# A hybrid decoder trunk on one core: token-major projections in wider passes, HGRN2 operands one step earlier, attention in one run, 1/rms turned by transfers

## The chip, the core and the metric

The kernel runs on one core of a Trainium2 chip. Five engines work side by side, each through its own queue of instructions in a fixed order: PE multiplies matrices into PSUM (eight banks of 128 partitions by 512 fp32 values), DVE works elementwise and reduces, ACT applies functions and copies with a scale, POOL fills constants and issues some of the transfers, SP issues the rest. The metric is the device time of one execution in microseconds, lower is better. A difference counts as measured from about 0.2%.

## The reference

Two layers over 512 tokens of width 1024, in fp32. Each layer has a half-step SwiGLU feed-forward, one combined projection whose columns feed three token mixers, one output projection, and a second half-step feed-forward:

```python
x = x + 0.5 * swiglu(rms_norm(x, ffn1_norm[l]), ffn1_w_in[l], ffn1_w_out[l])
h = rms_norm(x, mix_norm[l]) @ w_mix_in[l]
(c_x, c_b, c_c, h_q, h_f, h_i, h_g, f_q, f_k, f_v, f_f) = jnp.split(h, split_at, axis=-1)
y = jnp.concatenate([short_conv_mixer(...), hgrn2_mixer(...), fox_mixer(...)], axis=-1)
x = x + y @ w_mix_out[l]
x = x + 0.5 * swiglu(rms_norm(x, ffn2_norm[l]), ffn2_w_in[l], ffn2_w_out[l])
```

- The short convolution is causal, three taps over 256 channels: `b_gate * conv3(c_gate * x_in)`.
- HGRN2 has 4 heads of 64 by 64 and works in chunks of 64 tokens: a state per head decays by a forget gate per channel and takes up k v, and within a chunk every query sees earlier keys under the decay between them. Its output is normalised per head and multiplied by silu of a gate.
- FoX is causal attention with 8 heads of 64; q and k are normalised per head by their rms, the logits get the difference of cumulative log forget gates, and a softmax over the row follows.

## The kernel before

The residual stream stands in SBUF with features on partitions (`xT`, 8 tiles of 128 features by 512 tokens). Every fp32 operand of a dense product is split into a rounded high part (ACT, lines 334 and 732) and a low rest (DVE, lines 335 and 734), and a product is three matmuls: high by high, high by low, low by high (`mm3`, lines 346, 352, 353). The split weights stand in `hl`, of which there are three, filled from `st`, of which there are two. The norm's gain is in the operand; the factor 1/rms, `inv`, is applied to the products.

A dense product is streamed by `stream_steps`: two rows of weight tiles are loaded and split (a granule), multiplied for all accumulators (jobs), and then it yields, so that other work can be written between its steps. In the last granule it goes job by job, so that banks are finished one after the other.

The framework lists every engine's instructions by the order in which they are written and by its own estimate of when they are ready; `high_priority` lets the weight splits go ahead. The order on each engine is fixed when the program is built; dense matmuls can have been put ahead of a block that was written earlier and was not expected to be ready. PSUM's eight banks are named `mm` (three), `sc` (two), `pt` (two) and `po` (one), and a bank is given again when its readers are done.

The mixer of a layer (`mix`, line 926) runs like this:

1. Features by tokens: the forget logits, the gate and the q of HGRN2 (`features`, weights stationary, 512 tokens moving). The norm's sum is taken in the first one, and `inv` follows.
2. `inv` is also needed with tokens on partitions (`invc`, and `inv2` = `invc` squared over 64). Four one-column matmuls of `inv`'s first row with a 1 turn it (lines 997 to 1004).
3. HGRN2's v and the FoX forget logits, tokens by features, 264 columns in four banks (line 1019). `invc` scales them (lines 1027, 1030).
4. `hgrn` runs for two head pairs as two generators taken in turn. Its steps are gates, decayed keys, state sums and scan, then seven levels. At each level the elementwise operands `e` and `e2` are made, a block of fp32 matmuls gives the scores into an `sc` bank, and a masked copy (line 1290) puts them into `A`. Then follow the outputs in `po` (lines 1301, 1308) and their norm.
   Between these steps stand the steps of the FoX projections (`fox_qkv`): q, k and v of heads 0 to 3, then of heads 4 to 7, each a pass of 256 columns with two token blocks per bank (`tokens`), 4 steps of 24 matmuls. After q and k, each bank is squared, summed by head, and multiplied by its 1/rms out of PSUM (lines 1368 to 1376); v is split out of PSUM (lines 1382, 1383).
5. Attention, heads 0 to 3 (`fox_attend`), beside the convolution's projections (12 steps); then heads 4 to 7 as a new run, beside three quarters of the output projection (`most`, 12 steps). A head has four items, one for each block of 128 queries: scores three items ahead, softmax, transposes, products with V one item later. `beside` takes one dense step at each item from the third on, and what is left after the run. The order of the rows of the output projection is HGRN2 (2, 3), heads 0 to 3 (4, 5), convolution (0, 1), and after attention heads 4 to 7 (6, 7).

Loads of weights go by SP's queue. POOL's queue holds small loads at the mixer's start, the memsets of `q2` and of `S2` in HGRN2, and the ones for attention's operands.

## Time and profile before

| | us |
|---|---|
| median of 3 runs | 1847.46 (1845.98 to 1848.6) |
| the profiled execution | 1847.27 |
| its span | 1845.3 |
| granted TensorE clock | 1.0 throughout |
| projections beside HGRN2, layer 0 and layer 1 | 93.5 and 92.8 |
| attention, layer 0 and layer 1 | 110.2 and 110.4 |

A row of the table by windows gives a stretch, its length, and for each engine its busy time and its instructions. A row of the groups gives line, engine and operation, the tiles written and read, shape and count, then busy time, mean duration of one in ns, and the idle time ahead of them with what ended it. A row of the timeline gives start, duration, engine and line. A matmul's duration overlaps the next one's, so what one costs is read from start to start. The fp32 matmuls of HGRN2 stand as two rows each, so "x8" is a block of four.

### The profile page before, as it was taken

Reading aid. Unit: us, or ns where it says so; the run is one execution under the profiler, and the core shown is the slowest. Engines: PE = TensorE matmul, PEld = TensorE weight load, DVE = VectorE, ACT = ScalarE, POOL = GpSimd, SP = SyncE. Lnnn points to the kernel's source line nnn. Section 1 sums busy time; section 2 is a strip of 40 time slices with the busy share of each in tenths; the row PEclk is TensorE's granted clock in tenths of the full one; section 3 lists DMA queues with packets and bytes.
Section 4 is the critical chain, followed back from the end, with each engine's and each line's share of the span. In section 5 each row is a group of like instructions: output and inputs, shape, how many; then the busy total and the mean of one; then the engine's idle time right before and its main releaser. Section 6 shows DMA issues by size and latency. Waiting matters only on the chain.

```text
span 1845.3 us, 33378 instructions
## 1 busy us (share of the span) xinstructions
PE 1826.9 (99%) x13532; PEld 1698.6 (92%) x13532; DVE 1476.5 (80%) x2101; ACT 1005.9 (55%) x1462; POOL 182.5 (10%) x186
## 2 busy tenths in 40 slices
PE   8999999999999999999999999999999999999999
PEld 6899999899877899999889999998998788999997
DVE  7889787678787988879678887966868878888883
ACT  4455554564665555555445555545546665555552
POOL 0011120100000101112001111201000001020210
PEclk9999999999999999999999999999999999999999
DMA  7658783332323767868276787823323238677762
GB/s 205 183 126 194 178 177 92 69 96 72 76 75 98 215 136 175 186 169 172 81 201 139 169 188 184 172 61 89 81 64 87 81 103 228 151 158 195 150 137 91
DMA packets 247529, 254.00 MB, mean 138 GB/s; under 512 B 19632, under 2 KB 232112, under 8 KB 247376
## 3 DMA queue, kind: packets, MB, share of 16 engines
q1 hardware_dynamic: 191664, 183.69, 33.4%
q0 software_dynamic: 55712, 68.18, 23.2%
q8 instruction: 106, 1.74, 0.4%
q14 instruction: 47, 0.39, 0.1%
HBM read 226.08 MB, written 2.10 MB: 124 GB/s over the span
## 4 chain that ended last, share of the span: by engine, by line
PE 91%; DVE 4%; ACT 3%; issue 1%; DMA 1%; SPq 0%; ACTq 0%; DVEq 0%
PE mm L346 13%; PE mm L353 13%; PE mm L352 13%; PE sc L346 6%; PE sc L353 6%; PE sc L352 6%; PE pt L346 6%; PE pt L352 6%; PE pt L353 6%; PE po L346 3%; PE po L352 3%; PE po L353 3%; PE po L1449 1%; DVE hl L335 1%; ACT hl L334 1%
## 5 line engine op out<-in xcount | busy, mean ns | idle before, releaser
L732 ACT CAST hl<-w 128x1024 fp32r<-128x1024 f32 x322 | 337.7, 1050 | 346.9 <-PE mm L353 81.7
L734 DVE TENSOR_TENSOR hl<-w,hl 128x1024 fp32r<-128x1024 f32 x322 | 392.7, 1220 | 86.5 <-ACT hl L732 86.4
L335 DVE TENSOR_TENSOR hl<-st,hl 128x512 fp32r<-128x512 f32 (+2 forms) x196 | 166.5, 851 | 118.3 <-ACT hl L334 117.3
L334 ACT CAST hl<-st 128x512 fp32r<-128x512 f32 (+2 forms) x196 | 146.6, 750 | 206.9 <-PE mm L353 67.4
L346 PE MATMUL mm<-xc,hl 128*128 128x256 f32 (+1 forms) x730 | 201.3, 276 | 0.3 <-ACT g L831 0.3
L353 PE MATMUL mm<-xc,hl 128*128 128x256 f32 x728 | 201.2, 276 | 0.0
L352 PE MATMUL mm<-xc,hl 128*128 128x256 f32 x728 | 201.1, 276 | 0.0
L346 PE MATMUL sc<-xc,hl 128*128 128x256 f32 (+1 forms) x530 | 146.3, 277 | 0.6 <-ACT g L831 0.6
L353 PE MATMUL sc<-xc,hl 128*128 128x256 f32 x528 | 146.0, 277 | 0.0
L352 PE MATMUL sc<-xc,hl 128*128 128x256 f32 x528 | 145.9, 276 | 0.0
L346 PEld LDWEIGHTS mm<-xc,hl 128*128 128x128 f32 x730 | 137.1, 188 | 0.8 <-ACT g L831 0.5
L353 PEld LDWEIGHTS mm<-xc,hl 128*128 128x128 f32 x728 | 136.7, 188 | 0.1
L352 PEld LDWEIGHTS mm<-xc,hl 128*128 128x128 f32 x728 | 136.7, 188 | 0.0
L352 PE MATMUL pt<-xc,hl 128*128 128x256 f32 x480 | 132.6, 276 | 0.0
L346 PE MATMUL pt<-xc,hl 128*128 128x256 f32 (+1 forms) x482 | 132.6, 276 | 0.0
L353 PE MATMUL pt<-xc,hl 128*128 128x256 f32 x480 | 132.5, 276 | 0.0
L346 PE MATMUL mm<-hl,x 128*128 128x256 f32 (+1 forms) x384 | 112.4, 293 | 0.7 <-DVE ft L442 0.3
L346 PE MATMUL mm<-x,hl 128*128 128x512 f32 x272 | 109.7, 403 | 0.0
L353 PE MATMUL mm<-hl,x 128*128 128x256 f32 (+1 forms) x384 | 107.6, 280 | 0.0
L352 PE MATMUL mm<-hl,x 128*128 128x256 f32 (+1 forms) x384 | 107.3, 279 | 0.0
L353 PE MATMUL mm<-x,hl 128*128 128x512 f32 x272 | 106.5, 392 | 0.0
L352 PE MATMUL mm<-x,hl 128*128 128x512 f32 x272 | 106.0, 390 | 0.0
(470 smaller groups left out, 5677.1 us busy)
## 6 DMA issues: line engine op xcount, KB each, us to landing
w<-in_ffn_w_in_dram SPq DMA_DIRECT2D x140, 512.0 KB, 5.7
w<-in_ffn_w_out_dram SPq DMA_DIRECT2D x64, 512.0 KB, 4.4
w<-in_ffn_w_out_dram POOLq DMA_DIRECT2D x56, 512.0 KB, 8.9
st<-in_w_mix_in_dram SPq DMA_DIRECT2D x88, 256.0 KB, 2.7
w<-in_ffn_w_in_dram POOLq DMA_DIRECT2D x39, 512.0 KB, 8.4
st<-in_ffn_w_in_dram SPq DMA_DIRECT2D x72, 256.0 KB, 3.3
w<-S POOLq DMA_DIRECT2D x35, 512.0 KB, 4.7
st<-in_ffn_w_out_dram SPq DMA_DIRECT2D x24, 512.0 KB, 4.1
```

The lines of the kernel that those rows point to most:

```text
L334: a = nc.scalar.copy(hi, src[:, c : c + w])
L335: b = nc.vector.tensor_sub(lo, src[:, c : c + w], hi)
L346: i = nc.tensor.matmul(acc[:, c], ah, bh[:, c], start=first and c.start == 0, stop=False, skip_group_check=True,)
L352: nc.tensor.matmul(acc, ah, bl, start=False, stop=False, skip_group_check=True)
L353: i = nc.tensor.matmul(acc, al, bh, start=False, stop=last, skip_group_check=True)
L732: A(nc.scalar.copy(hi, src))
L734: return lambda: V(nc.vector.tensor_sub(lo, src, hi))
L1449: nc.tensor.matmul(self.ob[:, t0 + u * P : t0 + 2 * P], V[:, j, h % 4].rearrange("p a d -> p (a d)"), part[:, j, u:, :].rearrange("p i t - ...
```

## The change

- `stream_steps` gets `wide`: the first granule goes job by job as the last one does, and every granule yields in its middle too.
- `tokens` makes one pass of 512 columns over four banks (three `mm` and `po`), one token block in each: q and k of heads 0 to 3 together, q and k of heads 4 to 7, then v of all heads. Each pass has 4 granules of 48 matmuls with 512 moving columns, 8 half-passes in all.
- `fox_qkv` copies a bank of q and k to SBUF with ACT and squares, sums and scales it there. The square goes to a new tile `fs`, of which there is one.
- `hgrn` makes a level's operands one step earlier, behind the matmuls of the level before. Its output accumulates in an `sc` bank, not `po`.
- `invc` comes by two POOL transfers: `inv`'s first row to a DRAM tile, and from there one value a partition. The four matmuls and `ones_r` go.
- `fox_attend` runs once over eight heads. One generator gives the convolution's steps and then those of `most`; a step is taken at the stopping points listed in `BESIDE`. The run stops once more after the first head's preparation and once before its last products. The output projection takes the convolution (0, 1) second and heads 0 to 3 (4, 5) third.

```diff
--- before.py
+++ after.py
@@ -21,6 +21,8 @@
 BANKS = {"mm": 3, "sc": 2, "pt": 2, "po": 1}
 LOOK, LAG = 3, 1
+BESIDE = {0, 1, 2, 33} | {4 + (29 * n) // 20 for n in range(20)}
 P = 128
 T = 512
 D = 1024
@@ -198,6 +200,9 @@
...
+        self.dram = ctx.enter_context(
+            tc.tile_pool(name="dram", bufs=1, space=bass.MemoryType.DRAM)
+        )
...
@@ -216,8 +221,6 @@
...
-        self.ones_r = c.tile([1, 1], F32, tag="ones_r", name="ones_r")
-        nc.vector.memset(self.ones_r, 1.0)
...
@@ -358,7 +361,8 @@
         for _ in self.stream_steps(*args, **kw):
             pass
-    def stream_steps(self, jobs, parts_of, act, nk, mid=None, pre=None, deal=None, keep=False):
+    def stream_steps(self, jobs, parts_of, act, nk, mid=None, pre=None, deal=None, keep=False, wide=False):
@@ -383,12 +387,14 @@
             end = k + kk == nk
             order = (
                 [(job, j) for job in jobs for j in range(kk)]
-                if end
+                if end or wide and k == 0
                 else [(job, j) for j in range(kk) for job in jobs]
             )
             for n, ((acc, cols, toks, *more), j) in enumerate(order):
                 if pre is not None and n == len(order) // 2:
                     pre(k, True)
+                if wide and n == len(order) // 2:
+                    yield
                 ah, al = act(k + j)
                 hi, lo = rows[j]
                 first, last = k + j == 0 and not more, end and j == kk - 1
@@ -967,14 +973,13 @@
...
-            def tokens(a, banks=("mm", "mm")):
-                bs = [self.bank(t) for t in banks]
-                jobs = []
-                for i in range(4):
-                    acc = bs[i // 2][:, 256 * (i % 2) : 256 * (i % 2) + 256]
-                    jobs.append((acc, slice(0, 256), TOK[i]) + ((False,) if i % 2 else ()))
-                yield from self.stream_steps(jobs, cols((a, 256)), self.xact, KD)
+            def tokens(*spans):
+                bs = [self.bank(t) for t in ("mm", "mm", "mm", "po")]
+                yield from self.stream_steps(
+                    [(bk, slice(0, T), t) for bk, t in zip(bs, TOK)], cols(*spans),
+                    self.xact, KD, wide=True,
+                )
                 return bs
             with tc.tile_pool(name=self.n("hg"), bufs=1) as hp:
@@ -994,14 +999,10 @@
...
-                ib = self.bank("pt")
-                for i in range(4):
-                    nc.tensor.matmul(
-                        ib[:, i : i + 1], inv[0:1, TOK[i]], self.ones_r[0:1, 0:1],
-                        start=True, stop=True,
-                    )
                 self.invc, self.inv2 = col("invc", 4), col("inv2", 4)
-                nc.vector.tensor_copy(self.invc, ib[:, 0:4])
+                row = self.dram.tile([1, T], F32, tag="row", name=self.n("row"))
+                nc.gpsimd.dma_start(row, inv[0:1, :])
+                nc.gpsimd.dma_start(self.invc, row.rearrange("o (i p) -> (o p) i", p=P))
...
-                half = [{}, {}]
-                def projections():
-                    for hf in range(2):
-                        yield from self.fox_qkv(mp, hf, tokens, half)
-                dense = projections()
+                half = []
+                dense = self.fox_qkv(mp, hp, tokens, half)
                 step = 0
...
-                def beside(attend, dense):
-                    for n, _ in enumerate(attend):
-                        if n >= 2:
-                            next(dense, None)
-                    for _ in dense:
-                        pass
                 self.begin_norm(next_gain)
-                order = [2, 3, 4, 5, 0, 1, 6, 7]
+                order = [2, 3, 0, 1, 4, 5, 6, 7]
...
-                beside(self.fox_attend(ap_, 0, half[0], qkg), conv())
-                beside(self.fox_attend(ap_, 1, half[1], qkg), most())
+                def dense():
+                    yield from conv()
+                    yield from most()
+                g = dense()
+                for n, _ in enumerate(self.fox_attend(ap_, half, qkg)):
+                    if n in BESIDE:
+                        next(g)
+                    if n == max(BESIDE):
+                        next(g, None)
...
-        yield
         A = own("A", [P, 2, 4, P])
         A8 = A.rearrange("p h i t -> p (h i) t")
+        halves = lambda lev: lambda a, i: a.rearrange(
+            "p (n two w) -> p n two w", two=2, w=2**lev // 2
+        )[:, :, i, :]
+        def operands(lev):
+            w, half = 2**lev // 2, halves(lev)
+            e = tmp()
+            if lev == 0:
+                nc.vector.tensor_mul(e, q, k)
+                return e, None
+            if lev == 1:
+                self.act(half(e, 1), half(lf, 1), AF.Exp)
+                nc.vector.tensor_mul(half(e, 1), half(e, 1), half(q, 1))
+                nc.vector.tensor_mul(half(e, 0), half(e, 1), half(k, 0))
+                return e, None
+            n2 = T // (2 * w)
+            ref = b.rearrange("p (n s) -> p n s", s=2 * w)[:, :, w - 1 : w].to_broadcast(
+                [P, n2, w]
+            )
+            nc.vector.tensor_add(half(e, 0), half(kb, 0), ref)
+            nc.vector.tensor_sub(half(e, 1), half(b, 1), ref)
+            self.act(e, e, AF.Exp)
+            e2 = tmp().rearrange("p (h t) -> p h t", h=2)
+            nc.vector.tensor_mul(
+                e2.rearrange("p h (n w) -> p h n w", w=w),
+                half(e, 1).unsqueeze(1).to_broadcast([P, 2, n2, w]),
+                q2.rearrange("p h (n two w) -> p h n two w", two=2, w=w)[:, :, :, 1, :],
+            )
+            return e, e2
+        ready = operands(0)
+        yield
         for lev in range(7):
-            w = 2**lev // 2
-            half = lambda a, i: a.rearrange("p (n two w) -> p n two w", two=2, w=w)[:, :, i, :]
-            e = tmp()
+            w, half = 2**lev // 2, halves(lev)
+            e, e2 = ready
+            sb = self.bank("sc")
             if lev < 2:
...
                 for i in range(4):
                     nc.tensor.matmul(
                         sb[:, i:8:4], e[:, i * P : (i + 1) * P], self.heads2, start=True, stop=True
                     )
                 d = sb[:, :8].unsqueeze(2)
+                ready = operands(lev + 1)
                 if lev == 0:
                     nc.vector.tensor_mul(
                         A8, self.ident.unsqueeze(1).to_broadcast([P, 8, P]), d.to_broadcast([P, 8, P])
@@ -1265,35 +1291,21 @@
                         )
                 yield
                 continue
...
...
+            if lev < 6:
+                ready = operands(lev + 1)
...
-        ob = self.bank("po")
+        ob = self.bank("sc")
...
-    def fox_qkv(self, mp, hf, tokens, half):
-        nc = self.nc
...
+    def fox_qkv(self, mp, hp, tokens, half):
+        nc = self.nc
+        for hf in range(2):
+            qk = mp.tile([P, 4, 4, 2, HD], F32, tag="qk", name=self.n("qk"), bufs=2)
+            banks = yield from tokens((F_Q + 256 * hf, 256), (F_K + 256 * hf, 256))
+            for i, bank in enumerate(banks):
+                out = qk[:, i].rearrange("p h w d -> p w h d")
+                nc.scalar.copy(out, bank.rearrange("p (w h d) -> p w h d", w=2, h=4))
+                sq = hp.tile([P, 8, HD], F32, tag="fs", name=self.n("fs"))
+                s8 = lambda tag: mp.tile([P, 8], F32, tag=tag, name=self.n(tag), bufs=2)
                 m, r, t = s8("fm"), s8("fr"), s8("ft")
-                nc.scalar.activation(out, src, AF.Square)
-                nc.vector.reduce_sum(m, out, axis=AX.X)
-                bc = lambda c: c[:, 2 * bi : 2 * bi + 2].unsqueeze(2).to_broadcast([P, 2, 4])
-                nc.vector.tensor_mul(m, m, bc(self.inv2))
+                nc.scalar.activation(sq, qk[:, i].rearrange("p h w d -> p (h w) d"), AF.Square)
+                nc.vector.reduce_sum(m, sq, axis=AX.X)
+                nc.vector.tensor_scalar(
+                    m, m, scalar1=self.inv2[:, i : i + 1], scalar2=None, op0=ALU.mult
+                )
                 self.act(r, m, AF.Ln, bias=self.epsc)
                 self.act(r, r, AF.Exp, scale=-0.5)
                 self.rsqrt(r, m, r, t)
-                nc.vector.tensor_mul(r, r, bc(self.invc))
-                nc.vector.tensor_mul(out, src, r.unsqueeze(3).to_broadcast([P, 2, 4, HD]))
...
+                nc.vector.tensor_scalar(
+                    r, r, scalar1=self.invc[:, i : i + 1], scalar2=None, op0=ALU.mult
                 )
-        half[hf] = qk, V
+                out = qk[:, i].rearrange("p h w d -> p (h w) d")
+                nc.vector.tensor_mul(out, out, r.unsqueeze(2).to_broadcast([P, 8, HD]))
+            half.append(qk)
+        V = mp.tile([P, 4, NH, 2, HD], F32R, tag="V", name=self.n("V"))
+        for i, bank in enumerate((yield from tokens((F_V, T)))):
+            src = bank.rearrange("p (h d) -> p h d", d=HD)
+            sc = self.invc[:, i : i + 1]
+            nc.scalar.activation(V[:, i, :, 0, :], src, AF.Copy, scale=sc)
+            nc.vector.scalar_tensor_tensor(
+                out=V[:, i, :, 1, :], in0=src, scalar=sc, in1=V[:, i, :, 0, :],
+                op0=ALU.mult, op1=ALU.subtract,
+            )
+        half.append(V)
     def fox_prep(self, pool, h, qk, g):
@@ -1415,9 +1433,10 @@
         )
         return QA, QB, KA, KB
-    def fox_attend(self, pool, hf, qkv, g):
-        nc = self.nc
-        qk, V = qkv
+    def fox_attend(self, pool, half, g):
+        nc = self.nc
...
-                        V[:, j, h % 4].rearrange("p a d -> p (a d)"),
+                        half[2][:, j, h].rearrange("p a d -> p (a d)"),
...
         late = []
-        heads = range(4 * hf, 4 * hf + 4)
-        items = [(h, i) for h in heads for i in range(4)]
-        ops = {heads[0]: self.fox_prep(pool, heads[0], qk, g)}
-        pb = {it: scores(ops[heads[0]], it[1]) for it in items[:LOOK]}
+        items = [(h, i) for h in range(NH) for i in range(4)]
+        prep = lambda h: self.fox_prep(pool, h, half[h // 4], g)
+        ops = {0: prep(0)}
+        yield
+        pb = {it: scores(ops[0], it[1]) for it in items[:LOOK]}
         for n, (h, i) in enumerate(items):
             yield
-            if i == 0 and h + 1 in heads:
-                ops[h + 1] = self.fox_prep(pool, h + 1, qk, g)
+            if i == 0 and h + 1 < NH:
+                ops[h + 1] = prep(h + 1)
             if n + LOOK < len(items):
                 h2, i2 = items[n + LOOK]
                 pb[h2, i2] = scores(ops[h2], i2)
@@ -1495,8 +1515,10 @@
...
+        yield
         for a in late:
             values(*a[1:])
```

More of the change, by code (lines that the diff above doesn't have):

```diff
@@ L1267, in hgrn @@
                 continue
-            n2 = T // (2 * w)
-            ref = b.rearrange("p (n s) -> p n s", s=2 * w)[:, :, w - 1 : w].to_broadcast(
-                [P, n2, w]
-            )
-            nc.vector.tensor_add(half(e, 0), half(kb, 0), ref)
-            nc.vector.tensor_sub(half(e, 1), half(b, 1), ref)
-            self.act(e, e, AF.Exp)
-            e2 = tmp().rearrange("p (h t) -> p h t", h=2)
-            nc.vector.tensor_mul(
-                e2.rearrange("p h (n w) -> p h n w", w=w),
-                half(e, 1).unsqueeze(1).to_broadcast([P, 2, n2, w]),
-                q2.rearrange("p h (n two w) -> p h n two w", two=2, w=w)[:, :, :, 1, :],
-            )
-            sb = self.bank("sc")
             s2 = sb.rearrange("p (h t) -> p h t", h=2)
@@ L1355, in fox_decay @@
         )
-    def fox_qkv(self, mp, hf, tokens, half):
+    def fox_qkv(self, mp, hp, tokens, half):
         nc = self.nc
-        qk = mp.tile([P, 4, 4, 2, HD], F32, tag="qk", name=self.n("qk"), bufs=2)
-        for w, a in enumerate((F_Q, F_K)):
-            for bi, bank in enumerate((yield from tokens(a + 256 * hf, ("mm", "po" if w and not hf else "mm")))):
-                src = bank.rearrange("p (i h d) -> p i h d", i=2, h=4)
-                s8 = lambda tag: mp.tile([P, 2, 4], F32, tag=tag, name=self.n(tag), bufs=2)
-                out = qk[:, 2 * bi : 2 * bi + 2, :, w, :]
-                m, r, t = s8("fm"), s8("fr"), s8("ft")
-                nc.scalar.activation(out, src, AF.Square)
-                nc.vector.reduce_sum(m, out, axis=AX.X)
-                bc = lambda c: c[:, 2 * bi : 2 * bi + 2].unsqueeze(2).to_broadcast([P, 2, 4])
-                nc.vector.tensor_mul(m, m, bc(self.inv2))
+        for hf in range(2):
[6 more added lines that the diff above has]
+                s8 = lambda tag: mp.tile([P, 8], F32, tag=tag, name=self.n(tag), bufs=2)
+                m, r, t = s8("fm"), s8("fr"), s8("ft")
+                nc.scalar.activation(sq, qk[:, i].rearrange("p h w d -> p (h w) d"), AF.Square)
[3 more added lines that the diff above has]
+                )
                 self.act(r, m, AF.Ln, bias=self.epsc)
```

16 lines of the change are left out of this document (removed).

## The prediction

> **What bounds the kernel now.** I read the page first, its engine line and its chain of work.
>
> ```profile
> PE 1826.9 (99%) x13532; PEld 1698.6 (92%) x13532; DVE 1476.5 (80%) x2101; ACT 1005.9 (55%) x1462; POOL 182.5 (10%) x186
> ...
> PE 91%; DVE 4%; ACT 3%; issue 1%; DMA 1%; SPq 0%; ACTq 0%; DVEq 0%
> ```
>
> PE is both the busiest engine and the chain. So only two things are worth time: matmuls that go away or issue faster, and stretches where PE waits or issues slower than it can. Next I cut the mixer into stretches with the table by windows: projections beside HGRN2 (389 to 483 in layer 0, 1299 to 1392 in layer 1), then attention (483 to 593, 1392 to 1503).
>
> ```profile
> core 0: us, PE busy (x) PEld busy (x) DVE busy (x) ACT busy (x) POOL busy (x), PEclk, DMA share, GB/s
> 389.15:482.69 93.54, 92.05 (x835) 88.48 (x834) 71.14 (x158) 49.00 (x106) 1.86 (x4) 1.00 0.27 69
> 482.69:592.88 110.19, 108.74 (x610) 88.26 (x609) 90.10 (x197) 74.53 (x167) 4.32 (x8) 1.00 0.34 94
> 1299.32:1392.15 92.83, 91.54 (x834) 88.18 (x833) 70.74 (x158) 48.44 (x105) 1.86 (x4) 1.00 0.27 69
> 1392.15:1502.58 110.43, 109.20 (x611) 88.21 (x609) 90.20 (x198) 74.83 (x167) 4.31 (x8) 1.00 0.33 94
> ...
> 403.00:436.00 33.00, 31.93 (x273) 31.42 (x272) 30.51 (x70) 18.38 (x37) 1.86 (x4) 1.00 0.27 68
> 533.00:553.00 20.00, 19.62 (x119) 15.08 (x117) 18.61 (x42) 14.95 (x36) 1.04 (x2) 1.00 0.22 67
> ```
>
> Both layers look alike, so I work out layer 0 and double it. The clock is full everywhere. PE has no idle to speak of (1.5 us in each half), but the last two rows show where another engine comes close: DVE is busy 30.5 of 33 us in the middle of HGRN2 and 18.6 of 20 us around the seam between the two attention runs. The waits of PE in the HGRN2 stretch say the same, all of them on DVE:
>
> ```profile
> PE sc L1287 <- DVE t L1278: 0.8, 2, 0.4
> PE sc L1287 <- DVE fm L1371: 0.3, 1, 0.3
> PE mm L346 <- DVE ft L442: 0.2, 1, 0.2
> PE mm L346 <- DVE qk L1376: 0.2, 1, 0.2
> ```
>
> They sum to 1.5 us a layer.
>
> **The change part by part,** per layer.
>
> 1/rms by transfers. The four one-column matmuls on PE go:
>
> ```profile
> 365.24 0.39 PE L353 MATMUL po<-x,hl 128*128 128x512 f32 x1
> 365.55 1.05 PE L999 MATMUL pt<-ones_r,inv 1*128 1x1 f32 x8
> 366.53 0.50 PE L346 MATMUL mm<-x,hl 128*128 128x512 f32 x1
> ```
>
> From the start of the last matmul before to the first one after is 1.29 us, where the next one would have followed after about 0.23 (12 of them take 2.81, below). That is -1.1. In their place stand two POOL transfers, one waiting for the other; POOL holds nothing behind them but memsets that are needed tens of us later. The nearest row is the small column load on the same queue:
>
> ```profile
> cw<-in_conv_w_dram POOLq DMA_DIRECT2D x6, 1.0 KB, 3.2
> ...
> 355.36 0.69 DVE L446 TENSOR_TENSOR inv<-nr,nt 128x512 f32<-128x512 f32 x1
> ...
> 388.78 0.47 ACT L1027 ACTIVATE v<-mm,invc 128x256 f32<-128x256 f32 x1
> ```
>
> Two in a row are 6.4 us; inv is written at 356.1 and the column form is first read for v at 388.8. The cover is 32.7 us, so I cost the transfers at nothing. What could be late next is the small DVE product inv2 right behind them, if it stands too early in DVE's queue; the weight splits behind it would wait. That is a rival.
>
> Passes of 512 columns. The 24 steps of 24 narrow matmuls become 24 half-passes of 12 wide ones with the same number of multiplications. Here are two narrow steps between HGRN2 blocks, and a wide step between attention items:
>
> ```profile
> 431.45 0.36 PE L346 MATMUL mm<-hl,x 128*128 128x256 f32 x1
> ...
> 434.36 1.06 PE L1287 MATMUL sc<-t,t 128*128 128x128 f32 x8
> 435.17 0.37 PE L346 MATMUL mm<-hl,x 128*128 128x256 f32 x1
> ...
> 438.00 1.05 PE L1287 MATMUL sc<-t,t 128*128 128x128 f32 x8
> ...
> 499.33 0.44 PE L346 MATMUL mm<-x,hl 128*128 128x512 f32 x1
> ...
> 502.14 0.38 PE L1490 MATMUL pt<-ident,P 128*128 128x128 f32 x2
> ```
>
> A narrow step takes 2.91 or 2.83 us, a wide one 2.81, the restart after a foreign block included in each. I take the middle, 2.87 - 2.81 = 0.06 for each of 24: -1.3, with ends of -2.4 (all as the slow ones) and 0. The wide row has the tokens as moving operand, while here the weights move; I assume the same rate.
>
> The Trainium skill, page "TensorE: Matmul & The Clock Gate", section "Back-to-back issue gap", gives N/2.4 + 2.5 ns when warm. By it 24 narrow matmuls take 2.62 us and 12 wide ones 2.59, so this part would be -0.7 and not -1.3; the rows are longer than both, as they hold the restart, and I keep them.
>
> A pass now fills all three mm banks and po, so the next pass needs what the last one has not yet given back. Both outer granules go bank by bank, so a bank is written last three banks before it is reused: 3/4 of a granule of two half-passes, 4.2 us, and at least one HGRN2 block of 0.81. It is freed by one ACT copy, for which the nearest row is the square it stands beside:
>
> ```profile
> L1368 ACT ACTIVATE qk<-mm 128x512 f32<-128x512 f32 x7 | 4.1, 591 | 2.4 <-PE mm L353 2.4
> L1369 DVE TENSOR_REDUCE fm<-qk 128x8 f32<-128x512 f32 x8 | 5.5, 682 | 3.5 <-ACT qk L1368 3.5
> L1371 DVE TENSOR_TENSOR fm<-fm,inv 128x8 f32<-128x8 f32 x8 | 1.3, 162 | 0.1
> L1376 DVE TENSOR_TENSOR qk<-mm,fr 128x512 f32<-128x512 f32 x7 | 4.8, 683 | 0.1
> L1272 DVE TENSOR_TENSOR t<-kb,b 128x256 f32<-128x256 f32 x10 | 4.1, 414 | 0.0
> L1278 DVE TENSOR_TENSOR t<-t,q 128x512 f32<-128x512 f32 x10 | 6.9, 687 | 1.9 <-ACT t L289 1.8
> L1290 DVE COPY_PREDICATED A<-lmask,sc 128x512 f32<-128x512 uint8 x10 | 8.4, 837 | 0.0
> ```
>
> At 0.6 us a copy fits that cover seven times; the eight copies a layer add 4.7 us to an ACT busy 49 of 93.5. I cost them at nothing; if ACT is held up behind a DVE result, PE waits at the pass's first bank. V now comes last and its banks need an ACT and a DVE reading each, while attention prepares its first head; the first product with V comes 12 us after that start, so nothing here either.
>
> Operands one step ahead. This takes the product L1278 out of the wait of L1287. DVE does the same work, so I credit half of the 1.5 us: -0.7, ends -1.5 and 0. Its price is a burst: DVE now normalises four banks at once. A bank is 0.68 + 5 x 0.16 + 0.68 = 2.2 us, so four are 8.7. Over the next two half-passes (2 x 3.66 = 7.3 us with their blocks) DVE also has two HGRN2 steps of 2 x 0.41 + 0.69 + 0.84 = 2.35 each. That is 13.4 us of work in 7.3, a backlog of 6.1, against a lead of one step for each head pair, 7.3 us. The lead covers it, barely; where it does not, dense matmuls can be put ahead of the block. Hence nothing in the sum and a rival below.
>
> One run of attention. The seam is between the last values of heads 2 and 4; a head in the steady part is beside it (PE alone, then the dense matmuls alone):
>
> ```profile
> 528.98:552.07 23.09, 22.71 (x135) 1.00 0.23 69
> 513.95:528.98 15.03, 15.03 (x86) 1.00 0.31 89
> ...
> 528.98:552.07 23.09, 14.57 (x51) 8.80 (x51) 2.74 (x4) 2.44 (x5) 1.00 0.23 69
> 513.95:528.98 15.03, 11.89 (x48) 8.73 (x48) 2.62 (x4) 2.17 (x4) 1.00 0.31 89
> ```
>
> The steady head is 48 dense (4 x 2.81 = 11.24) and 38 others, 3.79 us. At these rates the seam's 51 dense and 84 others take 11.9 + 8.4 = 20.3, not 23.1: 2.8 us are lost there, four items with no dense step to cover DVE. The change spreads 20 dense steps over its stopping points 4 to 31. But DVE's 90.1 us must then fit into some 107 with less slack in each stretch (84% throughout, where the seam has 93%), so I credit 2.0 of 2.8: -2.0, ends -2.8 and 0. The convolution's output is now needed second: its six DVE operations of 0.69 and two ACT ones of 0.6 are 5.3 us, beside one dense step and an item (2.81 + 0.95). Up to 1.6 us could show, which I leave to the upper end, since scores of later items can go first.
>
> Sum: -1.1 - 1.3 - 0.7 - 2.0 = -5.1 a layer, -10.2 for both. The profiled execution took 1847.27 us (span 1845.3 and 2.0 around it), 0.2 below the median of 1847.46. So 1837.1. All gains at their better ends: -7.8 a layer, 1831.7. Only the first term, and the convolution late: +0.5, 1848.3.
>
> **The rivals.**
> Slower: the backlog. If DVE's burst after each of the two QK passes is not covered and no dense work goes ahead, PE waits at the next level's block. For it: 30.5 of 33 us, and all four waits above are on DVE. Against: they are 0.2 to 0.4 us each with two banks at once. Without the wait term the gain is 8.8 us; over four bursts it is eaten at 2.2 us each. With 3.6 each, the price if half the lead is gone, 14.4 - 8.8 = +5.6: 1852.9.
>
> Attention gives nothing, since DVE at 84% everywhere makes PE wait as much in small pieces: 1841.1. For it, the seam shows that DVE, not order, costs the time.
>
> The change does not do what it says: width and lead give nothing as well (a narrow step at 2.83 is a wide one): only -2.2, 1845.1.
>
> The transfers are on the path: two slow landings (8.9 us is the median for large accumulating ones on that queue) with DVE waiting in its queue, 17.8 less two granules of lead (2 x 2.7) are 12.4 a layer: 1861.9 with the other gains.
>
> ```profile
> w<-in_ffn_w_out_dram POOLq DMA_DIRECT2D x56, 512.0 KB, 8.9
> ```
>
> The Trainium skill, page "SBUF — State Buffer", section "SBUF: two separate sides", speaks for this rival: descriptors of POOL's transfers wait while DVE holds the shared port, about 3.1 us instead of 0.62. By that rule two landings would be 6.4 + 5.0, still far inside the cover; no row here shows such a wait.
>
> **How the numbers follow.** Forecast 0.55 (own range 1831 to 1843.5), attention nothing 0.14, only the first term 0.08, backlog 0.18, transfers 0.05. A measurement here tells 0.2% from no change, 3.7 us, so faster is below 1843.8: 0.55 + 0.14 and a little of the third, 0.70. Same 0.10, slower 0.20. The range goes from 1830 (a little under the better ends, for the first head's start, which I did not credit) to 1851, just short of the backlog.
>
> **What would show it.** No one-column matmuls near 366, and the first v scaling still near 388. Half-passes of 12 in about 2.81. Waits of PE on DVE under 1.5 us in HGRN2, and none on ACT's bank copies. No stretch of attention with PE below the steady rate between heads 2 and 4. Wrong would be: a longer projection stretch with waits on DVE at the levels behind a pass, or many small waits in attention.

## The result: 7.0 us less, but not from where it was expected

The changed kernel takes 1840.79 us (median of 6 runs, 1839.53 to 1842.32), the kernel before 1847.80 (median of 6): a ratio of 0.9961, 95% interval 0.9951 to 0.9971. That is 7.0 us faster, inside the range given, 3.7 short of the 1837.1 forecast, and close to the 1841.1 of the rival "attention gives nothing". The profiled execution took 1839.53 us with a span of 1837.8. Its engine line and chain of work:

```profile
PE 1820.7 (99%) x12940; PEld 1668.8 (91%) x12940; DVE 1472.5 (80%) x2066; ACT 1011.6 (55%) x1446; POOL 184.9 (10%) x190
...
PE 92%; DVE 4%; ACT 2%; issue 1%; DMA 1%; SPq 0%; ACTq 0%; DVEq 0%
```

PE has 592 fewer matmuls and is still the bound. The profile after by stages (table by windows; the columns are as before: window, length, then busy time of PE, PEld, DVE, ACT and POOL). Projections beside HGRN2 and attention, layer 0 and layer 1:

```profile
387.71:478.63 90.92, 89.72 (x546) 74.27 (x545) 69.47 (x143) 52.03 (x101) 2.62 (x6) 1.00 0.24 70
478.63:596.74 118.11, 116.74 (x640) 93.92 (x639) 97.53 (x207) 81.35 (x175) 3.44 (x7) 1.00 0.31 88
1294.40:1384.81 90.41, 89.72 (x547) 74.28 (x545) 69.45 (x143) 51.92 (x101) 2.62 (x6) 1.00 0.24 70
1384.81:1502.77 117.96, 116.69 (x640) 93.95 (x639) 97.49 (x207) 81.36 (x175) 3.45 (x7) 1.00 0.31 89
```

The same attention stage of the kernel before, now with its output projection, from the first transposes of the first head to the last matmul on fy:

```profile
482.69:600.49 117.80, 116.16 (x642) 93.97 (x640) 95.36 (x205) 78.88 (x174) 4.32 (x8) 1.00 0.31 88
1392.16:1510.17 118.01, 116.59 (x642) 93.90 (x640) 95.45 (x206) 79.17 (x174) 4.31 (x8) 1.00 0.31 88
```

Stage by stage, in us, measured from PE start to PE start in the two traces:

| stage | before, layers 0 and 1 | after | difference |
|---|---|---|---|
| sum of the norm to the first transposes of HGRN2's keys | 38.19, 38.20 | 37.03, 36.97 | -1.16, -1.23 |
| projections beside HGRN2 | 93.54, 92.84 | 90.92, 90.41 | -2.62, -2.43 |
| attention and output projection | 117.80, 118.01 | 118.11, 117.96 | +0.31, -0.05 |

They sum to -7.2. Everything outside the mixers has the same code in all kernels here; between profiles the stretch between the two mixers still varies by 2.0 us (660.5 to 662.5), so below parts are compared by these stages, and whole kernels by medians.

The projections now run like a metronome. Two HGRN2 blocks with a wide half-pass between them, and two matmuls of the half-pass before (timeline of PE):

```profile
430.03 0.39 PE L355 MATMUL mm<-hl,x 128*128 128x512 f32 x1
...
431.39 0.39 PE L355 MATMUL po<-hl,x 128*128 128x512 f32 x1
...
431.85 1.05 PE L1297 MATMUL sc<-t,t 128*128 128x128 f32 x8
432.66 0.48 PE L349 MATMUL mm<-hl,x 128*128 128x512 f32 x1
...
435.48 1.05 PE L1297 MATMUL sc<-t,t 128*128 128x128 f32 x8
436.28 0.48 PE L349 MATMUL mm<-hl,x 128*128 128x512 f32 x1
```

Each block holds PE for 0.81, each half-pass for 2.82 (2.86 in the first levels). None of the four waits on DVE that the kernel before had here is left. One new wait stands in their place; it is all that the waits of PE list in this stage, first layer 0, then layer 1:

```profile
PE pt L1190 <- ACT t L292: 1.2, 1, 1.2
```

```profile
PE pt L1190 <- ACT t L292: 0.7, 1, 0.7
```

It was in no part of the prediction. The timeline of layer 0 around it, ACT first, then DVE, then PE:

```profile
385.75 0.47 ACT L1028 ACTIVATE v<-mm,invc 128x256 f32<-128x256 f32 x1
388.10 1.05 ACT L337 CAST hl<-st 128x1024 fp32r<-128x1024 f32 x1 [1.89 <-DMA st<-in_w_mix_in_dram]
389.06 0.83 ACT L1028 ACTIVATE v<-sc,invc 128x256 f32<-128x256 f32 x2
...
391.55 0.66 ACT L292 ACTIVATE t<-t 128x512 f32<-128x512 f32 x1
```

```profile
389.19 1.23 DVE L338 TENSOR_TENSOR hl<-st,hl 128x1024 fp32r<-128x1024 f32 x1 [2.13 <-ACT hl L337]
...
390.73 0.68 DVE L1182 TENSOR_TENSOR t<-b,kb 128x512 f32<-128x512 f32 x1
```

```profile
392.26 0.66 PE L1190 MATMUL pt<-ident,t 128*128 128x128 f32 x4 [1.20 <-ACT t L292]
```

ACT takes its instructions in order. At 386 its next one is the cast of a weight granule whose load has not landed; behind that stand the remaining v copies. DVE stands in the same way behind the low part of that granule, and only then computes the exponent of the second head pair's decayed keys (390.73), which ACT exponentiates at 391.55 and PE wants to transpose at 391.1. The kernel before has the same late load (its timeline, ACT and PE):

```profile
388.25 0.62 ACT L334 CAST hl<-st 128x512 fp32r<-128x512 f32 x1 [2.65 <-DMA st<-in_w_mix_in_dram]
...
391.97 0.63 ACT L289 ACTIVATE t<-t 128x512 f32<-128x512 f32 x1 [0.64 <-DVE t L1184]
...
392.66 0.66 PE L1192 MATMUL pt<-ident,t 128*128 128x128 f32 x4
```

There the transposes start right behind the exponential as well, but PE gets to them about 1.5 us later, so that it loses only some 0.2 us (its step in front of them takes 3.15 where the next one takes 2.91). The first gain brought PE there 1.2 us earlier, and the profile after runs 0.3 us ahead at this point; the cast starts only 0.15 earlier.

### The profile page after: what moved, and what is told of

It reads as the page before. It is cut to its first block, busy times and chain, and to the rows that moved or that the text cites. A ratio compares the mean times of both kernels' runs of the same rounds, so it can differ in the third digit from the quotient of the medians.

```text
span 1837.8 us, 32074 instructions
## 1 busy us (share of the span) xinstructions
PE 1820.7 (99%) x12940; PEld 1668.8 (91%) x12940; DVE 1472.5 (80%) x2066; ACT 1011.6 (55%) x1446; POOL 184.9 (10%) x190
## 3 DMA queue, kind: packets, MB, share of 16 engines
q0 software_dynamic: 55840, 68.19, 23.1%
## 4 chain that ended last, share of the span: by engine, by line
PE 92%; DVE 4%; ACT 2%; issue 1%; DMA 1%; SPq 0%; ACTq 0%; DVEq 0%
PE mm L349 13%; PE mm L356 13%; PE mm L355 13%; PE sc L349 6%; PE sc L356 6%; PE sc L355 6%; PE pt L349 6%; PE pt L355 6%; PE pt L356 6%; PE po L349 4%; PE po L355 4%; PE po L356 4%; DVE hl L338 1%; ACT hl L337 1%; PE sc L1297 1%
## 5 line engine op out<-in xcount | busy, mean ns | idle before, releaser
L338 DVE TENSOR_TENSOR hl<-st,hl 128x1024 fp32r<-128x1024 f32 (+2 forms) x172 | 162.9, 949 | 131.5 <-ACT hl L337 131.0
L337 ACT CAST hl<-st 128x1024 fp32r<-128x1024 f32 (+2 forms) x172 | 142.0, 829 | 180.9 <-PE po L356 71.7
L349 PEld LDWEIGHTS sc<-xc,hl 128*128 128x128 f32 x530 | 99.5, 188 | 1.5 <-ACT g L837 1.0
L356 PEld LDWEIGHTS sc<-xc,hl 128*128 128x128 f32 x528 | 99.2, 188 | 0.1
L355 PEld LDWEIGHTS sc<-xc,hl 128*128 128x128 f32 x528 | 99.1, 188 | 0.0
```

The lines of the kernel that those rows point to most:

```text
L337: a = nc.scalar.copy(hi, src[:, c : c + w])
L338: b = nc.vector.tensor_sub(lo, src[:, c : c + w], hi)
L349: i = nc.tensor.matmul(acc[:, c], ah, bh[:, c], start=first and c.start == 0, stop=False, skip_group_check=True,)
L355: nc.tensor.matmul(acc, ah, bl, start=False, stop=False, skip_group_check=True)
L356: i = nc.tensor.matmul(acc, al, bh, start=False, stop=last, skip_group_check=True)
```

## The experiments

First each part of the change alone, in the kernel before. Each run has the kernel before beside it on the same chip (medians 1848.12, 1848.04 and 1849.57 in the three groups below). The changed kernel is in none of these groups, so the runs that start from it are held against it by their ratios to the kernel before, and by the stages of one profile each.

**Transfers alone.** The four one-column matmuls are replaced, nothing else.

```diff
-                    nc.tensor.matmul(ib[:, i : i + 1], inv[0:1, TOK[i]], self.ones_r[0:1, 0:1], ...)
-                nc.vector.tensor_copy(self.invc, ib[:, 0:4])
+                nc.gpsimd.dma_start(row, inv[0:1, :])
+                nc.gpsimd.dma_start(self.invc, row.rearrange("o (i p) -> (o p) i", p=P))
```

> The kernel before with one part alone: 1/rms turned by the two POOL transfers. If the terms add as in the traces (the stretch up to the first decayed-key transpose is 1.16 and 1.23 us shorter after the whole change), this alone gives -2.4 us. If the transfers, or the DVE product behind them, hold something up, the first v scaling stands later than 388.8 us and the gain is under 1 us.

Measured: 1846.79, ratio 0.9991 (0.9982 to 1.0): 1.3 of the expected 2.4, with an interval that reaches no change. The stage of the norm is 1.17 and 1.23 shorter, as expected; the projections behind it are 0.15 and 0.71 longer. In layer 0 the new wait on ACT is already there:

```profile
PE pt L1189 <- ACT t L290: 0.5, 1, 0.5
```

**Wide passes alone.** Narrow passes become passes over four banks; two runs of attention, operands as before.

```diff
-                    acc = bs[i // 2][:, 256 * (i % 2) : 256 * (i % 2) + 256]
+                bs = [self.bank(t) for t in ("mm", "mm", "mm", "po")]
```

> The kernel before with the wide passes alone (q and k copied out of PSUM, v of all heads last, HGRN2's output in an sc bank); HGRN2's operands stay where they were and attention stays in two runs. By width alone: -2.6 us for both layers. Rival: the wait of PE at the second decayed-key transposes that the trace after shows (1.2 and 0.7 us) comes with the larger loads of the wide passes, and the old waits on DVE stay; then the gain is about -2.6 + 1.9 = -0.7 us, and that wait stands in this trace.

Measured: 1845.97, ratio 0.9988 (0.998 to 0.9997). That is 2.15 less, nearer to the 2.6 by width than to the rival's 0.7, but the rival's wait on ACT is there. Projections -1.57 and -0.84, attention +0.01 and +0.22. Waits of PE in the projections of layer 0:

```profile
PE sc L1283 <- DVE ft L447: 0.6, 1, 0.6
PE pt L1188 <- ACT t L289: 0.4, 1, 0.4
PE sc L1283 <- DVE t L1274: 0.3, 1, 0.3
```

**Operands one step ahead alone.**

```diff
+        ready = operands(0)
+            e, e2 = ready
...
+                ready = operands(lev + 1)
```

> The kernel before with HGRN2's operands one step ahead alone. If the old waits of PE on DVE in the levels are the order of the operands, they go: -1.5 us a layer, -3.0 in all. If they are DVE's load (30.5 of 33 us), half of them stay: -1.5 in all or less.

Measured: 1848.30, ratio 1.0 (0.9992 to 1.0009): nothing, where 1.5 or 3.0 were expected. The waits on the products are gone, and one of the same size stands elsewhere:

```profile
PE mm L346 <- DVE V L1397: 1.3, 1, 1.3
```

That is a narrow pass waiting for a bank that DVE has still to empty of V; the step takes 4.33 us where its like take 2.91. The projections are 0.53 and 0.13 shorter than before; without these 1.4 us it would be 1.95 and 1.6. In the kernel before V of the first half comes in the middle of the passes, and DVE, which now does the products first, reaches it later. In the changed kernel V comes last, so this wait has no place there.

**One run of attention alone.**

```diff
-                beside(self.fox_attend(ap_, 0, half[0], qkg), conv())
-                beside(self.fox_attend(ap_, 1, half[1], qkg), most())
+                for n, _ in enumerate(self.fox_attend(ap_, half, qkg)):
+                    if n in BESIDE: next(g)
```

> The kernel before with attention in one run alone (steps at the listed stopping points, convolution second in the output projection). Theory: the time that the seam lost comes back as small losses in every head, since a head with three dense steps leaves PE 12 us where DVE has 10 to 11 us of work: 0 us, within 1. Rival: the join is worth its 2 us a layer, and the change loses it because v comes last in the wide passes; then -4 us here.

Measured: 1850.69, ratio 1.0015 (1.0006 to 1.0024), 2.6 slower, which neither the theory nor its rival had. Projections -0.42 and -0.05, attention +2.06 and +0.70. Two waits of PE are new, here in layer 0; the second is there in layer 1 too:

```profile
PE sc L348 <- ACT fyh L1469: 1.6, 1, 1.6
...
PE mm L348 <- DVE V L1387: 0.4, 1, 0.4
```

The 1.6 is again ACT standing at a cast for a late load, now of the FFN's weights, with the copy behind it that the last rows of the output projection need:

```profile
591.16 1.05 ACT L336 CAST hl<-st 128x1024 fp32r<-128x1024 f32 x1 [3.51 <-DMA st<-in_ffn_w_in_dram]
592.23 0.58 ACT L1465 COPY t<-po 64x512 f32<-64x512 f32 x1
```

Neither wait was taken away by itself in this kernel, so their part in its 2.6 is read from the trace only. The four parts alone sum to -1.33 - 2.15 + 0.18 + 2.57 = -0.7, each with an interval of about 1.7 to either side, where the whole change gives -7.0. They are not terms that can be added: the lead alone uncovers the wait on V, and the one run alone two waits that the whole change does not have. The wait on ACT that shows with the transfers and with the wide passes stays in the whole change.

Then the changed kernel with one thing taken back or mended. **Two runs of attention** in the changed kernel, the rest kept:

```diff
-                for n, _ in enumerate(self.fox_attend(ap_, half, qkg)): ...
+                beside(self.fox_attend(ap_, 0, (half[0], half[2]), qkg), conv())
+                beside(self.fox_attend(ap_, 1, (half[1], half[2]), qkg), most())
```

> The changed kernel with its attention put back into two runs, in the order of the kernel before; the transfers, the wide passes and the operands one step ahead stay. Theory: the loss at the seam only moved into small waits on VectorE, so one run is worth nothing here: 1840.8 within 1.5. Rival 1: the seam's loss did go (2 us a layer) and something else ate it, so two runs are 4 slower: 1845. Rival 2: one run costs what it cost alone (2.6 us), so two runs are faster: 1838.

Measured: 1841.25, ratio 0.9962 (0.9949 to 0.9974), beside 0.9961 for the changed kernel. Attention is 117.92 and 117.85, against 118.11 and 117.96. One run is worth nothing.

**The order of the two casts given.** The second granule of the first pass is cast behind the last v copy, the third behind the exponential of the second pair's decayed keys. Only these two dependencies are added, and on ACT and DVE only the instructions around them change places.

```diff
+                (F_Q + 256 * hf, 256), (F_K + 256 * hf, 256), after={} if hf else {2: "v", 4: "kd"}
...
+            if after is not None:
+                self.tc.add_manual_dep(a.ins, self.last[after], NOSYNC, reason="given order")
```

> The changed kernel, with the order of two weight casts on ScalarE given: the second granule's cast behind the four v copies, the third's behind the exponential of the second head pair's decayed keys. In the trace of the changed kernel this cast waits 1.89 us for its load in front of them, and TensorE's transposes wait 1.2 us (layer 0) and 0.7 us (layer 1). Theory: the in-order queue is what costs these 1.9 us, so they go: 1838.9. Rival: the late load is needed by the next wide step anyway, so the wait only moves there: 1840.8.

Measured: 1837.39, ratio 0.9945 (0.9932 to 0.9957). That is 3.4 less than the changed kernel by the medians and 3.0 by the ratios, whose intervals overlap a little; the stages tell it better. The projections are 89.51 and 89.53, which is 1.41 and 0.88 less: 2.3 in both. The three kernels here that have the casts ordered and the lead kept give 89.50 to 89.53 in all six of these stages. PE has no listed wait left in this stage of either layer. ACT and PE at the place:

```profile
388.61 0.47 ACT L1030 ACTIVATE v<-mm,invc 128x256 f32<-128x256 f32 x1 [0.25 <-PE mm L358]
388.99 1.04 ACT L337 CAST hl<-st 128x1024 fp32r<-128x1024 f32 x1
...
390.53 0.63 ACT L292 ACTIVATE t<-t 128x512 f32<-128x512 f32 x1
```

```profile
391.61 0.60 PE L1193 MATMUL pt<-ident,t 128*128 128x128 f32 x4
```

The half-pass between the two groups of transposes takes 2.84 instead of 4.20. Only the order was changed, so the wait is shown to come from the order of a queue, and the weights are not needed earlier than they come.

**No softmax scaling on VectorE** in three of four items; this kernel leaves out the normalisation of these rows:

```diff
-            nc.vector.reciprocal(rs, rs)
-            if i == 3: ... else: nc.vector.tensor_scalar(pb[:, :n], pb[:, :n], scalar1=rs, ...)
+            if i == 3: nc.vector.reciprocal(rs, rs); ...
```

> The changed kernel without the reciprocal and the scaling of P on VectorE in three of four attention items (the softmax of those rows stays unnormalised: this part of the computation is left out). That takes 8.3 + 24 x 0.16 = 12 us a layer from VectorE's 90. Theory (VectorE is what makes TensorE wait in attention): about half of the 4.3 us of waits that stand outside the steady rhythm go, 2 a layer: 1836.8. Rival (the loss is TensorE's own restarts between foreign matmuls, whatever VectorE does): no change, 1840.8.

Measured: 1840.76, ratio 0.9961 (0.9948 to 0.9973): no change. The same work scaled on ScalarE for the third item only, in the changed kernel:

```diff
-            if i == 3:
+            if i >= 2:
                 nc.scalar.activation(pb[:, :n], pb[:, :n], AF.Copy, scale=rs)
```

> The changed kernel with P of the third item of each head scaled on ScalarE, as it already is for the fourth: 8 x 0.42 = 3.4 us a layer from VectorE to ScalarE (8 x about 0.6). Theory (VectorE is what TensorE waits for): 0.3 to 1 us a layer less, 1839 to 1840. Rival (the length of the chain from score to P counts, and ScalarE's multiply is longer than VectorE's): 1841 to 1843.

Measured: 1840.08, ratio 0.9960 (0.9946 to 0.9974); attention is 0.42 shorter in each layer, too little for the medians to tell. The windows of attention in the kernel without scaling:

```profile
480.65:598.24 117.59, 116.21 (x641) 93.99 (x639) 88.78 (x159) 81.43 (x175) 3.34 (x7) 1.00 0.32 89
1386.12:1503.87 117.75, 116.27 (x641) 93.85 (x639) 88.89 (x159) 81.36 (x175) 3.36 (x7) 1.00 0.32 89
```

DVE is 8.7 us less busy than in the changed kernel (97.5) and the stage is 0.2 to 0.5 shorter. How much DVE has to do sets at most a small part of attention's time. What PE waits for in the changed kernel's attention is this (layer 0):

```profile
PE pt L1510 <- DVE KB L1430: 0.6, 2, 0.3
PE pt L1510 <- DVE PL L1513: 0.2, 1, 0.2
PE po L1468 <- DVE PL L1513: 0.2, 1, 0.2
PE sc L1446 <- ACT P L292: 0.2, 1, 0.2
```

The wait on KB comes twice, at heads 2 and 6. KB is the last reader of the pt bank in which a head is prepared, and these are the two heads whose second item has no dense step in front of it. In the kernel without the scaling, where DVE has less to do, this wait stays (0.5 us in layer 0, here, and 0.6 in layer 1):

```profile
PE pt L1508 <- DVE KB L1430: 0.5, 2, 0.3
```

So, with the casts ordered, **two dense steps moved by one item**:

```diff
-BESIDE = {0, 1, 2, 33} | {4 + (29 * n) // 20 for n in range(20)}
+BESIDE = {0, 1, 2, 33} | {
+    4, 5, 6, 8, 10, 11, 12, 14, 15, 17, 18, 19, 21, 22, 24, 26, 27, 28, 30, 31}
```

The old set has 9 and 25 where the new one has 10 and 26.

> The kernel with the two casts ordered (1837.4), with two of the 24 places of a dense step in attention moved by one item: the one before the first item of heads 2 and 6 goes to before their second item, so that every head's preparation, which holds one of the two pt banks until VectorE has written KB, is followed by a dense step. Theory (a held pt bank makes TensorE wait, 0.3 us at each of these two heads, whatever VectorE's load): 0.6 a layer goes, 1836.2. Rival (the waits move to the items that lose their dense step): 1837.4 within 0.5.

Measured: 1837.79, ratio 0.9938 (0.9926 to 0.9951), against 0.9945 with the casts alone: the intervals overlap, and by the medians nothing is told. The stage says more: 117.39 and 117.08 instead of 118.32 and 117.83, that is -0.93 and -0.75, and the wait on KB is gone from both layers.

**All three together**: casts ordered, two steps moved, the third item scaled on ScalarE (the three edits shown above).

> The two casts ordered, the two dense steps moved, and the third item of each head scaled on ScalarE. If the three are independent: 1837.4 - 1.2 - 0.7 = 1835.5. If attention is bound by TensorE's own stream and only the casts count: 1837.4 within 0.7.

Measured: 1835.10, ratio 0.9928 (0.9914 to 0.9942), faster than both kernels and clear of the changed kernel's interval. In attention no PE wait is left in the list of either layer (windows of attention, columns as above):

```profile
477.64:594.39 116.75, 116.45 (x640) 93.85 (x639) 94.40 (x199) 84.91 (x183) 3.45 (x7) 1.00 0.31 89
1381.46:1498.02 116.56, 116.25 (x640) 93.87 (x639) 94.40 (x199) 84.90 (x183) 3.45 (x7) 1.00 0.32 90
```

PE is busy 116.45 of 116.75 us in layer 0, and the stage still takes 116.75 and 116.56. The kernel before was only 1.05 and 1.45 above that.

**Operands not ahead**, casts ordered, all else as changed:

```diff
-            e, e2 = ready
+            nc.vector.tensor_add(half(e, 0), half(kb, 0), ref)
+            nc.vector.tensor_sub(half(e, 1), half(b, 1), ref)
+            self.act(e, e, AF.Exp)
...
-                ready = operands(lev + 1)
```

> The kernel with the two casts ordered, but HGRN2's operands built in the step that uses them, as in the kernel before. Theory (with wide passes VectorE's normalisation comes in bursts of four banks, and the lead keeps them off the blocks): the waits of TensorE on the products come back, at least the 0.9 to 1.5 us a layer that stand in the traces with narrow or wide passes alone: 1839.2 to 1840.4. Rival 1 (the lead is worth nothing, as when it was put in alone): 1837.4. Rival 2 (the bursts hit the blocks in full, two passes of 3.6 us a layer): about 1851.

Measured: 1842.37, ratio 0.9964 (0.9952 to 0.9977), above the 1839.2 to 1840.4 expected and far from the rival's 1851. Projections 91.32 and 91.34, that is +1.81 in each layer, twice what the listed waits say (both layers alike):

```profile
PE sc L1288 <- DVE ft L453: 0.6, 1, 0.6
PE sc L1288 <- DVE t L1279: 0.3, 1, 0.3
```

The rest is in the rhythm. Number of dense matmuls between consecutive blocks of the levels 2 to 6, layer 0, and the time that they take, counted in the two traces:

```
not ahead   13 3.46 | 27 7.02 | 9 2.16 | 12 2.82 | 7 1.72 | 7 1.72 | 10 2.38 | 11 2.61 | 13 3.04   blocks 0.81 to 0.91
one ahead   12 2.82 each time                                                                   blocks 0.81
```

Where a block is late, dense matmuls go ahead of it, so PE does not idle; but the blocks then cut into half-passes and take up to 0.1 longer each. Over the ten blocks that is 1.3 us more for the dense matmuls, the 0.9 of listed waits among them, and 0.4 more for the blocks.

## Why the prediction was right and wrong

The sign and the range held; the sum came near by errors that cancel. Per layer, mean of both:

| step | forecast | measured | by |
|---|---|---|---|
| 1/rms by transfers | -1.1 | -1.2 | stage of the norm |
| wide passes | -1.3 | -1.6 to -1.85 | wide alone -1.2 and the 0.4 wait on ACT; not-ahead kernel against before |
| operands ahead | -0.7 | -1.8 | the kernel with ordered casts, with and without them |
| one run of attention | -2.0 | +0.1 | the stage; two runs in its place: no difference |
| a wait on ACT | not seen | +1.15 | the two casts ordered |

With -1.85 for the wide passes the column sums to -3.6, or -7.2 for both layers. That this is the measured sum proves nothing more: the projections' three rows are differences along one chain, before, not ahead, casts ordered, changed kernel, and must add up. Put in in another order, the parts have other sizes, as the four runs of parts alone show.

*Transfers.* Right, and so was their cover. The second waits for the first, as said; the landings are 1.6 and 3.0 us, and the column form is there at 361.59 without DVE waiting for it, 24 us ahead of the first v copy at 385.75 in the fence above.

```profile
row<-inv POOLq DMA_DIRECT2D x2, 2.0 KB, 1.6
invc<-row POOLq DMA_DIRECT2D x2, 2.0 KB, 3.0
```

So the rival "transfers on the path" falls. The rule of the Trainium skill, page "SBUF — State Buffer", section "SBUF: two separate sides", on descriptors of POOL's transfers held back while DVE has the port, speaks of 3.1 us instead of 0.62 for one transfer. These landings sum to 4.6 us, less than half of the 6.4 + 5.0 that the prediction worked out by it; whether a wait for the port is part of them cannot be told here, and with 24 us of cover it would not show in the time.

*Wide passes.* The mechanism is right, with a half-pass at 2.82 to 2.87 where the row in attention gave 2.81. In the levels, where no wait disturbs them, narrow steps take 2.91 and 2.82 in turn: 0.045 more than a half-pass, 1.1 for 24, against the 1.3 of the forecast. The banks are free in time: no wait on an ACT bank copy is listed. What was left out is that the wide pass also took away part of the waits on DVE (1.5 listed before, 0.9 with wide passes alone). The granted clock is 1.00, and matmuls of 512 columns follow each other every 0.227 us (six of them from 430.03 to 431.39 in the fence above). The estimate by the Trainium skill, page "TensorE: Matmul & The Clock Gate", section "Back-to-back issue gap", was -0.7 for this part, with 0.216 us a matmul. That section gives the formula for a single isolated matmul, and about 0.131 us for 512 columns in a sustained stream. The trace agrees with neither figure; so the restart is not the only reason why the rows are longer than the estimate, as the prediction had it.

*Operands ahead.* The sized step that failed is "I credit half of the 1.5 us". The list of waits is not the whole cost of a late block: dense matmuls that go ahead of it hide the wait but not the disorder, and both went, 1.8 in all. With narrow passes the lead comes to about the same, 1.95 and 1.6, if the wait on V is set aside, which is read from the trace and not tried. The backlog rival falls by the same runs: with the lead the burst of four banks leaves no wait, and without it the stage loses 1.8, not the 3.6 after each pass; of the backlog of 6.1 that was worked out no more than that shows.

*One run of attention.* Here a step was wrong, not only its size: "At these rates the seam's 51 dense and 84 others take 11.9 + 8.4 = 20.3, not 23.1: 2.8 us are lost there". The rate of the others came from a single head, the last one of its run. No next head is prepared beside it, so it has none of the transposes of q and k that the seam has (groups of the seam's window in the kernel before):

```profile
L1401 PE MATMUL pt<-ident,qk 128*128 128x128 f32 x12 | 1.8, 274 | 0.0
```

And the counts of a window take in matmuls that overlap its edges: 34 others begin in that head and 80 in the seam, not 38 and 84. With 3.78 / 34 = 0.1112 us for each, the seam's loss is already 2.3 and not 2.8. A test was at hand: at these rates the whole stage would be 335 x 0.2342 + 304 x 0.1112 = 112.3 (dense matmuls and others, counted in the trace), 5.5 us less than it takes, with PE waits listed for 1.5 of them. From start to start a dense matmul of this stage takes 0.246 us on average and another one 0.117; in the best version, with no listed wait, they still take 0.241 and 0.119. So the rates of that head were not reached in any run here, with or without waits. Taking away every listed wait won 1.05 and 1.45 us in all (the best version against the kernel before), not 2.8 at one place. The rival that hit, "attention gives nothing", was right in its number and wrong in its reason: it put the loss on DVE's load, and 8.7 us less of that load changed the stage by 0.2 to 0.5. What could be taken away in the one run was mostly order: two heads are prepared with no dense step before the next transposes, and moving the two steps won 0.93 and 0.75 us. Scaling the third item on ACT won 0.4 in the changed kernel and 0.6 and 0.5 on top of that.

*The wait on ACT.* The prediction looked at ACT's busy share (49 of 93.5 us) and at its bank copies, and asked only of DVE's queue what stands behind a late operand. To its own question of what could be late next it named DVE's product inv2, which was in time, and not the loads: PE came 1.2 us earlier by the first part of the change and they did not.

Still open: by the medians ordering the casts gave 3.4 us, by the ratios 3.0, by the two stages 2.3; the rest is about as much as the stretches outside the mixers vary. And that the wait on a late load explains the whole loss of the one run put in alone is read from its trace, not tried.

## What to carry to other kernels

An edit that makes PE arrive earlier pays only as far as everything else arrives earlier too: look in the in-order queues at that place for an instruction that waits for a load, and at what stands behind it; a cast moved behind the work that is ready cost nothing here and gave as much as a whole part of the change. A list of waits gives a lower bound of what a late operand costs when other work can go ahead of it. And before a rate taken from one good stretch is used to call another stretch lossy, use it on the whole stage: if it leaves several times the listed waits unexplained, the rate is not that of the stage.

## What the runs showed that was not expected

Four parts that alone give -0.7 us give -7.0 together. Taking 8.7 us of 97.5 from the second busiest engine of a stage in which it is busy 83% of the time changed the stage by 0.2 to 0.5 us. And PE can be listed with 0.9 us of waits and still lose 1.8 in a stage, because blocks that come late are overtaken and cut into half-passes.
